# Loading the residual stream from one DMA queue instead of two, at the start of a fused decoder layer

## The chip, the cores and the metric

The kernel runs on one core of one Trainium2 chip. The metric is the device time of one execution in microseconds (us). A profile of one execution lists every instruction and every DMA of that core; its times count from the start of the span, and MB are 10^6 bytes.

## What is computed

One layer of a decoder trunk on x of shape (1, 1024, 1024) in float32, D = 1024 and 1024 tokens:

```python
mod = silu(c) @ w_ada + b_ada                     # 6 vectors of D
sh1, sc1, ga1, sh2, sc2, ga2 = split(mod, 6)
h = rmsnorm(x, g_attn) * (1 + sc1) + sh1
proj = h @ w_in                                   # 2760 columns
out_a = dilated_mixture(qa, ka, va)               # 8 heads
out_b = sparse_attention(qi, ki, wi, qb, ckv)     # 8 heads, indexer and top-256
x = x + ga1 * (concat(out_a, out_b) @ w_out)
h2 = rmsnorm(x, g_ffn) * (1 + sc2) + sh2
x = x + ga2 * ((silu(gate) * up) @ w_down)        # gate, up = h2 @ w_gu
return rmsnorm(x, g_final)
```

Only the first lines bear on the change: the first modulation (sh1 and sc1), the norm of x, and the first columns of `h @ w_in`.

## The kernel before, in words

All tensors are float32. Products that need the precision are made of three matmuls over high and low parts (hh and hl of h, wh and wl of a weight); this is `mm3`, and L366, L367 and L368 are its three matmuls.

**The start, which the change touches.** ScalarE (`A` in the code, ACT in the profile) issues five small loads: c into `cc` (L229), then g_attn, g_ffn, kv_norm_g and b_ada into `gst` (L232 to L235). `load_half(1)` and then `load_half(0)` load the two halves of x, 512 tokens each, into a tile `xi` of 128 partitions. A half is four DMAs (`load_x`, L106 to L111), one for each group of 32 partitions, in the order 0, 2, 1, 3; each has 512 KB in 128 rows of 4 KB. The four are dealt out in turn to the engines named in a tuple: SyncE (SP) takes groups 0 and 1 of each half, ScalarE groups 2 and 3.

Behind that, SyncE alone issues what follows. `mod1_load(0)` (L276) is eight DMAs of 256 KB each, in rows of 1 KB, into the tile `va`: a quarter of the columns of w_ada that make sh1 and sc1. Then come the first two pieces of w_in (`wraw`, L209, 512 KB each in rows of 512 bytes), `mod1_load(1)` into `score` (eight DMAs of 256 KB), and, as the buffers come free, groups 2 and 3 and further pieces of w_in.

The computation over them: ScalarE makes silu(c) with one Exp (L239) behind its DMA issues. `norm_half` takes the sums of squares of a half of x, two of its four pieces on ScalarE (L264) and two on VectorE (L261), then the root (L144) and the scaling of `xi` by it, half 1 on VectorE (L269), half 0 on GpSimd (L271). `mod1(g)` multiplies silu(c) with group g of the weights on TensorE (L288), copies the sums from PSUM on ScalarE (`macc`, L291), adds them up on TensorE (L295), and VectorE finishes two columns each of `a1` and `s1` (L299, L301). `h_part(k, half)` transposes one column block of one half of x (L307), scales and shifts it on ScalarE (L309), and rounds it to `hh` (L310); the rest goes to `hl` (L312). `w_cols` makes `wh` of a piece of w_in on ScalarE (L212) and `wl` on GpSimd (L215). The first products over `hh` are those of the indexer (`qi_proj`).

**What sets the order.** Each engine works through its instructions in order, and a DMA issue that must wait holds up what stands behind it on the same engine. Which instruction stands where on an engine is planned before the run: the program is built under `tile.TileContext(nc, schedule_with_timeline_sim=True)`, which orders each engine's instructions along a simulated timeline, and it also places the semaphores. Only in some later places does the code fix an order by hand (`tc.issue_after`), as where the bits of the top-k search on VectorE alternate with the projections on TensorE.

After the start come the indexer's scores (L418 to L424), the top-k search on VectorE beside the other projections, the two kinds of attention, the output projection, and the FFN with its final norm. None of them is touched.

Of the kernel before, what the change touches and what calls it, by code (L numbers as in the profile page):

```python
# [68 lines left out]
def hybrid_block(ctx, tc, x, c, w_ada, b_ada, g_attn, w_in, kv_norm_g, w_uk, w_uv, w_out, g_ffn,  # L69
                 w_gu, w_down, g_final, lnm, out, dbg=None):  # L70
    nc = tc.nc
    V, A, G, PE = nc.vector, nc.scalar, nc.gpsimd, nc.tensor
# [32 lines left out]
    def load_x(engs, xi, t0, t1):  # L105

        for i, r in enumerate((0, 2, 1, 3)):
            src = bass.AP(tensor=x.tensor, offset=x.offset + (t0 * P + r) * D,
                          ap=[[4 * D, 32], [P * D, t1 - t0], [1, D]])
            last = engs[i % len(engs)].dma_start(xi[32 * r:32 * r + 32], src)  # L110
        return last  # L111
# [110 lines left out]
    xh = {}  # L222

    def load_half(half):
        xh[half] = stg.tile([P, 4, D], F32, name="xi", tag="xi", bufs=2)
        load_x((nc.sync, A), xh[half], half * 4, half * 4 + 4)

    cc = const.tile([P, 8], F32, name="cc")
    A.dma_start(cc, c.rearrange("b (p k) -> (b p) k", k=8))  # L229
# [4 lines left out]
    A.dma_start(gst[16:17], kv_norm_g)  # L234
    A.dma_start(gst[32:80], b_ada.rearrange("b (k p) -> (b k) p", p=P))  # L235
    load_half(1)
    load_half(0)
    ce = const.tile([P, 8], F32, name="ce")
    A.activation(ce, cc, AF.Exp, scale=-1.0)  # L239
# [1305 lines left out]
```

## Time and profile before

| | us |
|---|---|
| median of 3 runs | 1442.23 |
| lowest, highest | 1440.17, 1444.19 |
| the profiled execution | 1437.92 |
| its span, first to last instruction | 1436.1 |

The profile lists, for each engine, when an instruction ran and what ended the idle time before it. PE is TensorE's matmul, PEld its weight load, DVE VectorE, ACT ScalarE, POOL GpSimd; SPq and ACTq are instructions that issue DMAs on SyncE and ScalarE. In the view of the DMA queues, q1 is the queue that SyncE issues on and q10 the one of ScalarE; sixteen DMA engines serve both, and a packet is one row of a transfer.

### The profile page before, as it was taken

The numbers are of one execution on the slowest core, as the hardware profiler recorded it, in microseconds if no ns is written. First come the engines' busy times: TensorE is split into PE (matmuls) and PEld (weight loads), VectorE is DVE, ScalarE is ACT, GpSimd is POOL, SyncE is SP. The second block draws the span as 40 slices with busy tenths as digits, with TensorE's granted clock in tenths as the row PEclk, the third lists the DMA queues.
The fourth block names the chain that finished last, engine by engine and source line by source line (L and its number), as shares of the span: only waits on it lengthen the run. The fifth ranks groups of instructions, "written<-read, shape, count | busy, mean of one in ns | idle before, by whom it ended". The sixth has DMA issues, their size and how long they took to land.

```text
span 1436.1 us, 20358 instructions
## 1 busy us (share of the span) xinstructions
PE 1297.0 (90%) x7477; PEld 1033.9 (72%) x7477; DVE 1016.3 (71%) x1754; ACT 598.8 (42%) x1217; POOL 674.9 (47%) x454
## 2 busy tenths in 40 slices
PE   2999898999878899999869999999999998888894
PEld 0566776798666677787748888888888886766773
DVE  4136899999887477644987545554545569999997
ACT  3435546461456565613763333333333223223334
POOL 1650311324330598122676444445544436487865
PEclk9999898999989999999979999999999999999997
DMA  9723124233311444273423222222223281404004
GB/s 240 238 75 117 30 67 125 91 101 95 126 52 54 147 142 119 76 227 114 161 79 98 89 88 81 66 88 81 81 88 96 87 322 46 154 23 154 0 1 118
DMA packets 133018, 152.11 MB, mean 106 GB/s; under 512 B 9715, under 2 KB 95540, under 8 KB 132918
## 3 DMA queue, kind: packets, MB, share of 16 engines
q1 hardware_dynamic: 122160, 129.56, 29.8%
q0 software_dynamic: 4672, 15.73, 2.9%
q10 hardware_dynamic: 6086, 5.52, 1.5%
q8 instruction: 59, 0.97, 0.3%
q14 instruction: 41, 0.34, 0.1%
HBM read 115.65 MB, written 34.60 MB: 105 GB/s over the span
## 4 chain that ended last, share of the span: by engine, by line
PE 49%; DVE 29%; POOL 8%; DMA 6%; issue 5%; ACT 3%; SPq 1%; DVEq 0%; ACTq 0%; POOLq 0%
DVE score L620 7%; PE mm L1258 6%; PE mm L1256 6%; PE mm L1257 6%; PE tp L1256 3%; PE tp L1258 3%; PE tp L1257 3%; PE mm L366 3%; PE mm L368 3%; PE mm L367 2%; PE o L762 2%; DVE yacc L1376 2%; PE mm L762 2%; PE tp L762 2%; DVE score L424 2%
## 5 line engine op out<-in xcount | busy, mean ns | idle before, releaser
L1240 ACT ACTIVATE wo<-f 128x512 fp32r<-128x512 f32 x124 | 78.0, 631 | 178.0 <-PE mm L1258 78.8
L1241 DVE TENSOR_TENSOR wo<-f,wo 128x512 fp32r<-128x512 f32 x124 | 102.7, 831 | 43.8 <-ACT wo L1240 41.9
L366 PE MATMUL mm<-hh,wl 128*128 128x512 f32 (+2 forms) x288 | 111.7, 389 | 0.0
L367 PE MATMUL mm<-hh,wh 128*128 128x512 f32 (+2 forms) x288 | 111.2, 387 | 0.0
L368 PE MATMUL mm<-hl,wh 128*128 128x512 f32 (+2 forms) x288 | 108.1, 385 | 0.0
L214 POOL TENSOR_SCALAR wh<-wraw 128x1024 fp32r<-128x1024 f32 (+1 forms) x20 | 20.3, 1032 | 132.6 <-PE mm L368 82.3
L366 PE MATMUL mm<-wo,wo 128*128 128x512 f32 x148 | 59.0, 398 | 10.1 <-DVE wo L1366 10.1
L215 POOL TENSOR_TENSOR wl<-wraw,wh 128x1024 fp32r<-128x1024 f32 (+1 forms) x22 | 52.6, 2410 | 29.8 <-ACT ry L144 29.7
L366 PEld LDWEIGHTS mm<-hh,wl 128*128 128x128 f32 (+1 forms) x288 | 54.4, 189 | 15.2 <-issue 2.8
L368 PEld LDWEIGHTS mm<-hl,wh 128*128 128x128 f32 (+1 forms) x288 | 53.7, 188 | 14.0 <-issue 2.2
L367 PEld LDWEIGHTS mm<-hh,wh 128*128 128x128 f32 (+1 forms) x288 | 54.6, 190 | 11.5 <-issue 1.1
L368 PE MATMUL mm<-wo,wo 128*128 128x512 f32 x148 | 56.9, 393 | 1.7 <-DVE wo L1366 1.7
L367 PE MATMUL mm<-wo,wo 128*128 128x512 f32 x148 | 58.2, 393 | 0.0
L793 ACT ACTIVATE ttB<-ttB,mn 128x128 f32<-128x128 f32 (+7 forms) x64 | 49.1, 768 | 15.5 <-DVE mn L789 14.9
L1366 DVE TENSOR_TENSOR wo<-f,wo 128x1536 fp32r<-128x1536 f32 (+1 forms) x17 | 55.1, 3246 | 0.0
L1310 POOL TENSOR_TENSOR f<-f 128x512 f32<-128x512 f32 x15 | 19.8, 1322 | 74.2 <-ACT f L1309 74.2
L366 PE MATMUL mm<-wo,ml 128*128 128x512 f32 x128 | 51.6, 403 | 1.8 <-DVE ml L1109 1.8
L762 PE MATMUL tp<-ident,ttB 128*128 128x128 f32 x288 | 43.6, 294 | 10.2 <-ACT ptB L808 9.7
L620 DVE TENSOR_SCALAR_CACHE_REDUCE score<-kl,sc 128x1024 bf16<-128x1024 uint16 (+2 forms) x48 | 52.3, 1140 | 0.0
L620 DVE TENSOR_SCALAR_CACHE_REDUCE score<-ka,sc 128x768 bf16<-128x768 int16 (+2 forms) x48 | 52.3, 1139 | 0.0
L367 PE MATMUL mm<-wo,mh 128*128 128x512 f32 x128 | 51.0, 398 | 0.0
L368 PE MATMUL mm<-wo,mh 128*128 128x512 f32 x128 | 50.9, 398 | 0.0
(469 smaller groups left out, 4238.7 us busy)
## 6 DMA issues: line engine op xcount, KB each, us to landing
f<-in_w_gu_dram SPq DMA_DIRECT2D x44, 512.0 KB, 3.8
spg<-f POOLq DMA_DIRECT2D x44, 256.0 KB, 2.8
wraw<-in_w_in_dram SPq DMA_DIRECT2D x21, 512.0 KB, 4.0
f<-spg SPq DMA_DIRECT2D x33, 256.0 KB, 3.0
va<-in_w_ada_dram SPq DMA_DIRECT2D x16, 512.0 KB, 4.2
wlm<-in_w_ada_dram SPq DMA_DIRECT2D x32, 256.0 KB, 2.7
f<-in_w_down_dram SPq DMA_DIRECT2D x23, 256.0 KB, 3.1
more<-in_w_down_dram SPq DMA_DIRECT2D x21, 256.0 KB, 5.4
```

Source lines behind the costliest of these rows:

```text
L215: G.tensor_tensor(lo, raw, hi.bitcast(F32), op=OP.subtract)
L366: PE.matmul(p, al, bh, start=(j == 0), stop=False)
L367: PE.matmul(p, ah, bh, start=False, stop=False)
L368: PE.matmul(p, ah, bl, start=False, stop=(j == n - 1))
L620: V.tensor_scalar(mask(t, u), keys[:, seg[t]], z[:, i:i + 1], 0.0, op0=OP.is_lt, op1=OP.add, accum_out=cnt[:, i:i + 1])
L762: pe_last[0] = op(*args, **kw)
L1240: A.activation(h_, src, AF.Copy)
L1241: V.tensor_tensor(l_, src, h_.bitcast(F32), op=OP.subtract)
L1256: PE.matmul(p, w[1][:, k], a[0][:, k], start=(k == 0), stop=False)
L1257: PE.matmul(p, w[0][:, k], a[0][:, k], start=False, stop=False)
L1258: PE.matmul(p, w[0][:, k], a[1][:, k], start=False, stop=(k == 3))
L1366: V.tensor_tensor(l_, x, h_.bitcast(F32), op=OP.subtract)
```

## The change

The tuple of engines in `load_half` loses SyncE. All eight DMAs of x are issued by ScalarE, behind its five small loads, and SyncE's first DMA is the first one of `mod1_load(0)`. Sizes, order of the eight among themselves, tiles and everything else in the code stay.

```diff
     def load_half(half):
         xh[half] = stg.tile([P, 4, D], F32, name="xi", tag="xi", bufs=2)
-        load_x((nc.sync, A), xh[half], half * 4, half * 4 + 4)
+        load_x((A,), xh[half], half * 4, half * 4 + 4)
```

## Rows read from the trace of the kernel before

**Rows 1.** The page's head and its part on busy time: time, share, instructions
```profile
span 1436.1 us, 20358 instructions
PE 1297.0 (90%) x7477; PEld 1033.9 (72%) x7477; DVE 1016.3 (71%) x1754; ACT 598.8 (42%) x1217; POOL 674.9 (47%) x454
```

**Rows 2.** Windows: stretch, length, busy us of each engine, PEclk, DMA share, GB/s
```profile
0.00:36.00 36.00, 8.76 (x33) 2.47 (x33) 15.40 (x49) 11.46 (x18) 5.53 (x12) 0.98 1.02 240
36.00:110.00 74.00, 70.34 (x385) 47.31 (x384) 21.22 (x42) 29.37 (x51) 40.52 (x29) 0.98 0.54 162
```

**Rows 3.** Timeline of SyncE: start, us, engine, line, instruction, output and input, count
```profile
0.74 1.80 SPq L110 DMA_DIRECT2D xi<-in_x_dram  x4
6.04 20.03 SPq L276 DMA_DIRECT2D va<-in_w_ada_dram  x8
26.11 1.09 SPq L209 DMA_DIRECT2D wraw<-in_w_in_dram  x2
```

**Rows 4.** Timeline of ScalarE to 36 us; in brackets the idle time before, its releaser
```profile
5.75 0.32 ACTq L235 DMA_DIRECT2D gst<-in_b_ada_dram  x1
6.36 7.81 ACTq L110 DMA_DIRECT2D xi<-in_x_dram  x4
14.20 1.28 ACT L239 ACT_TABLE_LOAD   x1 [14.20 <-DMA gst<-in_b_ada_dram]
...
19.67 1.06 ACT L264 ACTIVATE sq<-xi 128x1024 bf16<-128x1024 f32 x1 [3.97 <-DMA xi<-in_x_dram]
...
25.22 1.06 ACT L264 ACTIVATE sq<-xi 128x1024 bf16<-128x1024 f32 x1 [1.84 <-DMA xi<-in_x_dram]
...
27.22 0.19 ACT L264 ACTIVATION_READ_ACCUMULATOR sq<-xi 128x1 f32 x1
30.71 0.60 ACT L291 ACTIVATE macc<-o 128x512 f32<-128x512 f32 x1 [3.31 <-PE o L288]
31.31 1.06 ACT L212 ACTIVATE wh<-wraw 128x1024 fp32r<-128x1024 f32 x1
...
33.10 1.06 ACT L212 ACTIVATE wh<-wraw 128x1024 fp32r<-128x1024 f32 x1 [0.64 <-DMA wraw<-in_w_in_dram]
34.06 0.76 ACT L309 ACTIVATE h<-tp,mcol 128x512 f32<-128x512 f32 x1
```

**Rows 5.** Who SyncE's issues waited for, to 80 us: total us, times, longest
```profile
SPq L276 <- DMA xi<-in_x_dram: 6.3, 3, 2.2
SPq L276 <- DMA cc<-in_c_dram: 3.5, 1, 3.5
```

**Rows 6.** DMA queues from 6 to 12 us: packets, MB, share of 16 engines
```profile
q1 hardware_dynamic: 327, 1.21, 104.3%
q10 hardware_dynamic: 18, 0.00, 0.7%
```

**Rows 7.** DMA queues from 15 to 24 us
```profile
q10 hardware_dynamic: 453, 1.66, 82.5%
q1 hardware_dynamic: 449, 0.43, 23.4%
```

**Rows 8.** DMA queues from 36 to 50 us, weights alone
```profile
q1 hardware_dynamic: 5066, 4.88, 109.5%
```

**Rows 9.** Windows again: the first 3 us, and a stretch of w_in alone
```profile
0.00:3.00 3.00, 0.00 (x0) 0.00 (x0) 1.28 (x13) 0.00 (x0) 2.04 (x10) 1.00 0.37 62
30.00:33.00 3.00, 2.22 (x16) 1.31 (x12) 0.55 (x6) 1.75 (x3) 0.49 (x1) 1.00 1.16 297
```

**Rows 10.** Timeline of all engines around the first products
```profile
29.62 1.05 PE L288 MATMUL o<-va,tab 128*32 128x512 f32 x4 [0.48 <-DMA va<-in_w_ada_dram]
...
34.69 1.90 PE L288 MATMUL o<-score,tab 128*32 128x512 f32 x4 [1.78 <-DMA score<-in_w_ada_dram]
...
37.69 4.41 POOL L271 TENSOR_SCALAR xi<-xi,rr 128x1024 f32<-128x1024 f32 x4 [0.53 <-DVE rr L151]
```

**Rows 11.** Who TensorE waited for, whole span: total us, times, longest
```profile
PE tp L1186 <- DVE f L1179: 12.9, 2, 7.2
```

## The prediction, made before the changed kernel was run

> **What bounds the kernel now.** The page comes first: TensorE is busy for 1297.0 of 1436.1 us [rows 1], so a change at the start is worth what it moves the moment from which TensorE has work without a break. The windows view gives that moment: until 36 us TensorE is busy for 8.76 us while the DMA engines' share is 1.02, and from 36 to 110 us it is busy for 70.34 of 74 us [rows 2]. The start is bound by loads, what follows by TensorE, and a shift at 36 us reaches the end about one for one.
>
> The timelines of the two issuing engines show how the loads stand. SyncE issues its four DMAs of x from 0.74, then eight weight DMAs spread from 6.04 to 26.07, then w_in [rows 3]. ScalarE issues its four DMAs of x from 6.36 to 14.17, and only then loads the table for the Exp [rows 4]. The spreading is waiting: SyncE's weight issues waited 3.5 us for the landing of `cc` and 6.3 us in three waits for landings of x [rows 5]. I read it so that each issue waits for a DMA several places earlier to land, whichever queue that was on.
>
> The queue view gives three rates. From 6 to 12 us only q1 moves anything, x in 4 KB rows, 1.21 MB, or 0.202 MB/us; q10 gets 18 packets, though ScalarE issued x at 6.36 [rows 6]. From 15 to 24 us q10 carries x and q1 weights in 1 KB rows: 453 packets against 449, so one each in turn, and 1.66 against 0.43 MB, or 0.184 and 0.048 MB/us [rows 7]. Weights alone go at 4.88 MB in 14 us, 0.348 MB/us [rows 8]; w_in at 0.297 [rows 9]. So x is the slow kind, and beside weights it takes four fifths.
>
> **The change, part by part.** Sizes are from the code: x 8 x 512 KB = 4.19 MB, first weights 8 x 256 KB = 2.10 MB, first w_in 2 x 512 KB = 1.05 MB. The same bytes must come; what changes is their order.
>
> Issues. SyncE loses four issues (1.80 us [rows 3]) that stand before all weights; ScalarE gets four more at idle time. I cost both at nothing: until 36 us TensorE waits for bytes. If that cover were gone, the price would be some 2 us.
>
> Weights start first. The first 3 us moved at 62 GB/s, 0.19 MB [rows 9], which at 0.202 MB/us puts the first bytes at 2.1 us. From there weights run alone until x joins. ScalarE's x waits behind its five small loads; it began at 6.36 because the fifth of these left only at 5.75 [rows 4]. Now the first four weight DMAs, 1.05 MB, are through at 2.1 + 1.05/0.348 = 5.1, the small loads among them. I take first bytes of x at 5.5 (bounds: 4, with the small loads landing at once, and 12, as before). By then 3.4 x 0.348 = 1.18 MB of weights are in.
>
> From 5.5 both flow as in rows 7. Half 1 takes 2.10/0.184 = 11.4 us, to 16.9, half 0 the same again, to 28.3. Before, q10 ran dry at about 24.1 and ScalarE squared half 0 at 25.22 [rows 4]; that lag of 1.1 us gives half 1 at 18.0 (19.67 before [rows 4]) and **half 0 at 29.4, against 25.2**. The other 0.92 MB of weights needs 0.92/0.048 = 19.2 us: in at 24.7, usable at 25.8, where the last matmul of the first modulation waited for them until 29.62 [rows 10]. Then w_in: about 0.1 MB beside the end of x, the other 0.95 MB at 0.297 in 3.2 us, to 31.5, usable at about 32.2 with a lag of 0.7, against 33.10 [rows 4]. The gain on bytes is 0.9 us.
>
> The added wait on ScalarE. Its last issue of x can leave only when the fourth DMA of half 1 has landed (18.0), and the table load stands behind it: 18.3 to 19.6, against 14.20 to 15.48 [rows 4]. Then the Exp, and the squares of half 1 from 19.8, where they stood at 19.67: no loss. The first modulation's matmuls wait for silu(c), at about 20.7; sixteen at 1.90/4 = 0.48 us [rows 10] end at 28.4, before ScalarE can use them, as follows.
>
> ScalarE works in order: squares of half 0, then `macc`, then two `wh`, then `h`. The squares took from 25.22 to 27.41, 2.19 us, and it then idled 3.31 us until `macc` [rows 4]. That idle time hides 3.3 us of a later half 0: up to a landing at 28.5 nothing moves, behind it all does. At 29.4 the squares end at 31.6, `macc` is 0.9 us later, the first `wh` starts at 32.2 and the second 1.15 us later (31.31 to 33.10 less the wait of 0.64 for w_in, which is gone [rows 4]), at 33.35; it takes 1.06, so `h` starts at 34.4 against 34.06: 0.3 us later. On the other side the second group's weights follow w_in and come 0.9 us earlier, and TensorE waited for them at 34.69 [rows 10]. GpSimd's `wl` stands behind `wh`, and its scaling of half 0 behind that: 37.69 [rows 10] becomes 38.6, 0.9 us later, and the transposes of half 0 wait for it.
>
> Sum: between 0.9 us gained on weights and 0.9 us lost through half 0. I take +0.3, the shift of `h`, which both paths meet. The profiled execution took 1437.92, its span and 1.8 us around; that makes 1438.2. The median is 4.3 us above that execution, and from it I forecast 1442.5. A measurement of this kernel can tell about 0.3% from no change, 4.3 us: this is none.
>
> [...]
>
> **The rivals.** *x comes later still: slower.* Place: half 0 in front of `macc` on ScalarE. It decides once half 0 lands after 28.5, and passes the 0.3% bound at 32.8. If the engines alternated by DMA instead of by packet, 512 KB of x to 256 KB of weights, x would get two thirds of 0.232, 0.155 MB/us, and 4.19 MB would take 27.0 us: 5.5 + 27.0 + 1.1 = 33.6, 5.1 us past the point, 1447. At worst SyncE's queue holds ScalarE's back, as rows 6 look: 2.10 MB of weights (6.0 us), w_in (3.5) and the second group (6.0) first, so x from 17.6, alone at 0.202 for 20.8 us, usable at 39.5: 11.0 us past the point, 1453. For it: rows 6. Against it: rows 7, with DMAs of both queues waiting and packets one for one. Chance 0.12. [...]
>
> *The weights' head start counts: a little faster.* If `macc` is planned before the squares of half 0, it runs when the matmuls end at 28.4, and the second `wh` waits for w_in alone, 0.9 us earlier. The rest of the path then gains that 0.9, 1441.3. For it: the plan orders by a simulated timeline, in which x and weights have moved. Against it: the order now, and GpSimd's late half 0. Chance 0.20, still within 0.3%.
>
> *The plan changes far from the start.* The order on every engine comes from that timeline; a shift of a microsecond at the start can exchange neighbours anywhere. One exchange costs or saves about a long wait of TensorE: the longest later one is 7.2 us [rows 11]. Faster: 1442.2 - 7.2 = 1435, chance 0.22. Slower: 1449.4, chance 0.08. For it: nothing in the code fixes the order at the start. Against it: TensorE is full from 36 us on, and a plan that is only moved in time keeps its order.
>
> *Nothing happens*: the same bytes by 32 us, whatever the queue. That is within the forecast.
>
> **The numbers.** Forecast 0.38 and the little gain 0.20 lie within 0.3%: same 0.58. Faster 0.22 is the changed plan. Slower 0.20 is late x with 0.12 and the changed plan with 0.08. The range holds the changed plan on both sides and the first price of a late x: 1435 to 1450. Only the held-back queue and larger changes of plan lie outside.
>
> **What would show it.** SyncE's first weight issue at 0.74, and q1 at 1 KB rows in the first 6 us; ScalarE's x from 4 to 5 us on, its last issue near 18, the table load behind it; q10 dry near 28; squares of half 0 on ScalarE near 29.4; `macc` near 31.6; TensorE's first product within 1 us of 36.5. If x starts near 12 or runs well under 0.184 MB/us, the sharing is wrong; if `macc` stands before the squares, the order is; if TensorE's start is right and the end is off by more than 2 us, the plan has changed further on.

## The result, and the profile after

| | before | after |
|---|---|---|
| median of 9 runs each, side by side (us) | 1440.17 | 1452.01 |
| lowest, highest (us) | 1436.80, 1450.86 | 1446.69, 1455.63 |
| the profiled execution (us) | 1437.92 | 1446.69 |

The ratio is 1.0068, 95% interval 1.0041 to 1.0095: slower by 0.68%, 9.8 us of 1442. It is estimated from the single executions, those more than 1.5% above the fastest of their kernel left out (here none), and is not the quotient of the two medians, 1.0082. The forecast was no change, and its range ended at 1450. The profiled execution of the changed kernel is the fastest of its nine, so its span understates the loss; the start, where the kernels differ, is what to read in it.

Two windows of the changed kernel (columns as in [rows 2]), then one of the kernel before, from the second of [rows 2]:

```profile
0.00:36.00 36.00, 4.53 (x17) 1.05 (x17) 4.79 (x26) 3.85 (x6) 3.21 (x11) 0.94 0.99 224
36.00:60.00 24.00, 19.36 (x73) 7.14 (x74) 13.10 (x31) 11.66 (x21) 10.76 (x8) 0.67 0.98 309
```

```profile
36.00:60.00 24.00, 23.56 (x118) 11.13 (x116) 3.62 (x9) 10.37 (x17) 15.38 (x12) 0.95 0.99 310
```

TensorE's busy time in the first 60 us falls from 32.32 to 23.89 us: 8.4 us of its work are pushed behind 60 us. Fewer bytes have come by 36 us (224 against 240 GB/s, 8.06 against 8.64 MB), and TensorE's clock is granted at 0.67 between 36 and 60 us. That is a mean of its two levels: after TensorE had stood idle from 28.43 us, the clock was at 0.50 from 31.5 to 51.9 us, and at 1.00 from there to 110 us.

Which moment carries the shift on? `hh` is the high part of `h` that the projections read, made in sixteen pieces. One row of it for the kernel before, then after (name, count, ns min/median/max, first and last start in us):

```profile
L310 ACT ACTIVATE hh<-h x16: 622/630/634, 34.9 to 78.2; 128x512 fp32r<-128x512 f32 x16
```

```profile
L310 ACT ACTIVATE hh<-h x16: 613/627/642, 47.4 to 88.9; 128x512 fp32r<-128x512 f32 x16
```

The first `hh` is 12.5 us later and the last 10.7. The first row of the top-k search (L620) starts at 200.5 us instead of 190.4, 10.1 us later. The loss is made before 90 us and then carried along.

Where does it come from? SyncE, ScalarE and VectorE in the changed kernel's timeline:

```profile
0.74 7.30 SPq L276 DMA_DIRECT2D va<-in_w_ada_dram  x8
8.86 11.76 SPq L209 DMA_DIRECT2D wraw<-in_w_in_dram  x2
21.20 16.62 SPq L276 DMA_DIRECT2D score<-in_w_ada_dram  x8
```

```profile
4.17 17.66 ACTq L110 DMA_DIRECT2D xi<-in_x_dram  x8
21.86 1.28 ACT L239 ACT_TABLE_LOAD   x1 [21.86 <-DMA xi<-in_x_dram]
...
33.64 1.06 ACT L212 ACTIVATE wh<-wraw 128x1024 fp32r<-128x1024 f32 x1 [10.28 <-DMA wraw<-in_w_in_dram]
34.60 1.04 ACT L264 ACTIVATE sq<-xi 128x1024 bf16<-128x1024 f32 x1
...
36.68 1.04 ACT L212 ACTIVATE wh<-wraw 128x1024 fp32r<-128x1024 f32 x1
37.63 0.57 ACT L291 ACTIVATE macc<-o 128x512 f32<-128x512 f32 x1
...
45.91 0.78 ACT L309 ACTIVATE h<-tp,mcol 128x512 f32<-128x512 f32 x1 [3.04 <-DVE ss L261]
```

```profile
35.77 2.50 DVE L261 CUSTOM_DVE_ANT_0 sq<-xi 128x1024 bf16<-128x1024 f32 x1 [10.27 <-ACT sq L264]
```

Set these beside [rows 3, 4]. SyncE sends all eight weight DMAs by 8.04 and the first piece of w_in at 8.86, and ScalarE's x starts behind its small loads and spreads to 21.83. And the planner has written **another order on ScalarE**: the first `wh` now stands ahead of all the squares, and `macc` behind the second `wh`. Half 1 of x has landed, but ScalarE waits 10.28 us for w_in; VectorE, which shares the squares, waits 10.27 us for ScalarE. TensorE (idle time and its releaser in brackets) had its first modulation done at 28.43, and then waited 9.82 us for `macc`; its first product starts at 48.12, not 36.5:

```profile
24.27 4.16 PE L288 MATMUL o<-va,tab 128*32 128x512 f32 x16 [14.55 <-DVE tab L281]
38.25 1.87 PE L295 MATMUL tp<-ones,macc 128*128 128x1 f32 x8 [9.82 <-ACT macc L291]
...
48.12 0.77 PE L366 MATMUL mm<-hh,wl 128*128 128x512 f32 x1 [1.07 <-ACT hh L310]
```

The chain of work that ended last says it near its start in three pieces (start, us, what), a single DMA being the long one:

```profile
3.10 5.74 DMA va<-in_w_ada_dram
8.86 24.76 DMA wraw<-in_w_in_dram
33.64 1.06 ACT wh L212
```

Two things have thus changed, the loads and ScalarE's order. Each could be the cause, and the low clock a third.

### The profile page after: what moved, and what is told of

Its sections match the earlier page's. It is cut to its first block, busy times and chain, and to the rows that moved or that the text cites. A ratio compares the mean times of both kernels' runs of the same rounds, so it can differ in the third digit from the quotient of the medians.

```text
span 1444.9 us, 20363 instructions
## 1 busy us (share of the span) xinstructions
PE 1301.7 (90%) x7477; PEld 1038.2 (72%) x7477; DVE 1015.5 (70%) x1754; ACT 598.5 (41%) x1217; POOL 676.1 (47%) x454
## 4 chain that ended last, share of the span: by engine, by line
PE 52%; DVE 31%; DMA 5%; POOL 4%; issue 4%; ACT 4%; SPq 0%; DVEq 0%; ACTq 0%; POOLq 0%
DVE score L620 7%; PE mm L1256 6%; PE mm L1257 6%; PE mm L1258 6%; PE o L762 3%; PE tp L1256 3%; PE tp L1258 3%; PE tp L1257 3%; PE mm L366 3%; PE mm L368 3%; PE mm L762 3%; PE mm L367 3%; PE tp L762 2%; DVE yacc L1376 2%; DVE wo L1366 2%
## 5 line engine op out<-in xcount | busy, mean ns | idle before, releaser
L366 PE MATMUL mm<-wo,wo 128*128 128x512 f32 x148 | 60.4, 408 | 8.6 <-DVE wo L1366 8.6
L368 PE MATMUL mm<-wo,wo 128*128 128x512 f32 x148 | 58.2, 402 | 1.7 <-DVE wo L1366 1.7
L367 PE MATMUL mm<-wo,wo 128*128 128x512 f32 x148 | 59.4, 401 | 0.0
L620 DVE TENSOR_SCALAR_CACHE_REDUCE score<-ka,sc 128x768 bf16<-128x768 int16 (+2 forms) x48 | 52.3, 1140 | 0.0
L620 DVE TENSOR_SCALAR_CACHE_REDUCE score<-kl,sc 128x1024 bf16<-128x1024 uint16 (+2 forms) x48 | 52.3, 1140 | 0.0
L424 DVE SCALAR_TENSOR_TENSOR score<-rl,wi,score 128x512 f32<-128x512 f32 (+2 forms) x70 | 48.3, 747 | 3.1 <-ACT rl L418 2.0
L367 PE MATMUL mm<-wo,mh 128*128 128x512 f32 x128 | 50.3, 393 | 0.0
```

Source lines behind the costliest of these rows:

```text
L366: PE.matmul(p, al, bh, start=(j == 0), stop=False)
L367: PE.matmul(p, ah, bh, start=False, stop=False)
L368: PE.matmul(p, ah, bl, start=False, stop=(j == n - 1))
L620: V.tensor_scalar(mask(t, u), keys[:, seg[t]], z[:, i:i + 1], 0.0, op0=OP.is_lt, op1=OP.add, accum_out=cnt[:, i:i + 1])
```

## The experiments

The letters of theories in an expectation are its own. The table has all twelve beside the changed kernel: the ratio to the kernel before, with its interval, and the start of the last `hh` in the profiled execution (78.2 before, 88.9 after).

| run | x on | ratio | last `hh` |
|---|---|---|---|
| the changed kernel | one queue | 1.0068 [1.0041, 1.0095] | 88.9 |
| squares first | one | 1.0032 [1.0011, 1.0053] | 83.2 |
| `macc`, `wh` first | one | 1.0100 [1.0067, 1.0133] | 86.4 |
| half 0 behind squares | one | 1.0103 [1.0068, 1.0138] | 90.5 |
| warm TensorE | one | 1.0088 [1.0065, 1.0111] | 88.5 |
| small loads moved, squares first | one | 0.9994 [0.9975, 1.0013] | 77.4 |
| small loads moved | one | 1.0003 [0.9987, 1.0019] | 77.6 |
| `wh` first | two | 0.9997 [0.9970, 1.0025] | 79.6 |
| order of after | two | 1.0015 [0.9991, 1.0038] | 81.0 |
| x before small loads | two | 1.0021 [0.9993, 1.0050] | 79.9 |
| small loads moved | two | 0.9983 [0.9966, 0.9999] | 72.3 |
| the same again | two | 0.9993 [0.9969, 1.0016] | 72.1 |
| same half at once | two | 1.0037 [1.0013, 1.0060] | 77.7 |

### Is it ScalarE's order? The order mended, the loads kept

The changed kernel, with both conversions of w_in collected and written behind the squares of half 0.

```diff
-    wqi = [w_cols([(C_QI, P), (C_QI + P, P)], True)]
+    converts = []
+    wqi = [w_cols([(C_QI, P), (C_QI + P, P)], True, converts)]
...
+    with tc.issue_after(sq_on_act[0].ins):
+        for convert in converts:
+            convert()
```

> x stays on ScalarE's queue alone; only ScalarE's order is changed back: the two conversions of w_in (wh) stand behind the squares of both halves of x. Theory A (the loss is the order that was planned on ScalarE: it waits for w_in from 23.4 to 33.6 us in front of the squares of half 1): the squares of half 1 start by 24, the first h by 36 instead of 45.9, and the time returns to 1440 to 1444 where the kernel before is at 1440, at least 6 us under the changed kernel. Theory B (the loss is the bytes: x and w_in land late, whatever the order): the first h stays above 42 and the time within 3 us of the changed kernel's, about 1450. Theory C (the loss is made by exchanged neighbours in later stages): the first h comes early, but the end stays some 8 us behind it.

Measured 1446.21 us, 1.0032: about half the loss is gone. The first `h` comes at 39.77, between the times that theories A and B name. ScalarE's timeline, and who TensorE waited for between 30 and 50 us (total, times, longest):

```profile
23.38 1.04 ACT L272 ACTIVATE sq<-xi 128x1024 bf16<-128x1024 f32 x1
...
28.86 0.60 ACT L299 ACTIVATE macc<-o 128x512 f32<-128x512 f32 x1 [3.31 <-PE o L296]
...
32.81 1.06 ACT L272 ACTIVATE sq<-xi 128x1024 bf16<-128x1024 f32 x1 [1.84 <-DMA xi<-in_x_dram]
...
34.91 1.99 ACT L214 ACTIVATE wh<-wraw 128x1024 fp32r<-128x1024 f32 x2
...
39.77 0.78 ACT L317 ACTIVATE h<-tp,mcol 128x512 f32<-128x512 f32 x1 [2.87 <-PE tp L315]
```

```profile
PE o L296 <- DMA score<-in_w_ada_dram: 4.5, 3, 3.1
```

`macc` comes even earlier than before (28.86 against 30.71), so weights ahead of x did pay there. But half 0 is squared 7.6 us later than before (32.81 against 25.22), and the second group of weights keeps TensorE waiting for 4.5 us. Which of the two decides, the chain that ended last tells:

```profile
15.73 19.81 DMA wraw<-in_w_in_dram
...
37.50 5.89 DMA score<-in_w_ada_dram
43.53 1.07 PE o L296 x4
```

It runs over w_in and not over x. SyncE's last issues of the second group stand behind the landing of w_in at 35.54, so the last four matmuls over that group start at 43.53, where they started at 40.19 in the kernel before. The last `hh` is 5.0 us late: that part is the loads'. The other 5.7 us came with the order.

### The order alone, with the loads of before

Two runs on the kernel before: the first conversion of w_in written ahead of the squares of half 1, with `macc` still in front; and the changed kernel's full order (`wh`, squares of half 1, `wh`, `macc`, squares of half 0).

```diff
+    first_wh = converts[0]()
...
-    norm_half(1)
+    with tc.issue_after(first_wh.ins):
+        norm_half(1)
+    converts[1]()
```

> The kernel before, x on both queues, with one thing taken from the changed kernel: on ScalarE the first conversion of w_in stands ahead of the squares of half 1. Theory A: the conversion can't start before w_in has landed (about 31 us in the kernel before), the squares move from 19.7 to about 32.4, the first h from 34.1 to 42 or 44, and the time rises by 6 to 10 us, to 1446 to 1450. Theory B: x and weights land as before, so the time stays within 2 us of 1440.

> x on both queues as before; ScalarE's order at the start is set by hand to the changed kernel's: first conversion, squares of half 1, second conversion, and only then the sums of the first modulation. Those sums then move from 30.7 to about 35 us, TensorE stands idle from 30.7 to 36 and its clock may fall as it did in the changed kernel. If this order is the larger part of the loss whatever the loads, the time rises by 4 to 7 us, to 1446 to 1449. If the loss needs both, late w_in and this order, it stays within 2 us of the kernel before.

Measured 0.9997 and 1.0015, neither distinguishable from 1. In the first, `h` starts 10 us late (44.35) at no cost that the time shows: TensorE runs the second group's modulation meanwhile, and the last `hh` starts at 79.6. The second puts `h` at 45.59, as late as in the changed kernel, and its last `hh` at 81.0, 2.8 us late instead of 10.7. So **a late first `h` is no measure of the loss**, and the order by itself explains about 2.8 us of lateness. In these profiled executions loads and order cost 5.0 + 2.8 = 7.8 us each alone and 10.7 together: about 3 us come only with both. That w_in is late just where the order waits for it would explain them; no run separates it.

The reverse was tried too, the changed kernel's loads with the first run's order (`macc`, `wh`, squares):

> x on ScalarE's queue alone; ScalarE's order at the start is set by hand to that of the second experiment (sums of the first modulation, then the first conversion, the squares of half 1, the second conversion, the squares of half 0), which cost nothing with x on both queues. If late bytes alone cost (theory B, the 0.3% that the first experiment kept), it comes out as the first experiment did, 1444 to 1447 where the kernel before is at 1442. If the place of the sums behind both conversions was what cost the rest, this order saves 3 to 6 us against the changed kernel. If instead any order with a conversion ahead of the squares costs when w_in lands at 33 us, it stays at 1449 to 1452.

The median is 1460.04, but its ten runs spread from 1444.74 to 1471.43, far wider than those of the changed kernel, and the profiled one was the fastest of them (last `hh` at 86.4). Why it spreads stays open. It does not rescue the change.

### Less beside each other: half 0 held back

The changed kernel, with half 0 of x and both conversions of w_in placed only behind the squares of half 1.

```diff
-    load_half(0)
...
+    with tc.issue_after(sq_on_act[1].ins):
+        load_half(0)
```

> x on ScalarE's queue alone, but half 0 is issued behind the squares of half 1, so the weights and w_in share the DMA engines with 2.1 MB of x instead of 4.2 first; the conversions of w_in stand behind the squares of half 1. Theory A with the loads as priced: half 1 lands by 18 to 20, w_in near 25, the first h by 32; half 0 lands only near 40 and its transposes follow. The time is 1436 to 1444. Theory B: the loss is x's lateness, half 0 is later than in the changed kernel, and the time is at or above 1450.

Measured 1.0103. `macc` gains (23.14 against 28.86), but half 0 is issued only from 30.68 to 34.01, though the squares of half 1 ended at 25.81: ScalarE idled 8.23 us until its next instruction, by the profile for a weight DMA. VectorE, which waits for half 0 itself, squares it at 47.58; ScalarE does at 50.86, behind two more `macc` that now stand ahead. Holding half 0 back in this way costs more than sharing did.

### Is it TensorE's clock?

The changed kernel with 70 small products of the identity behind the first modulation's, so that TensorE does not idle there.

```diff
+        if g == 0:
+            warm = mm_tile("mm")
+            for j in range(70):
+                with tc.issue_after(last_mod.ins):
+                    last_mod = PE.matmul(warm[:, :P], ident, ident, start=True, stop=True)
```

> The changed kernel with 70 small matmuls of the identity added on TensorE behind the first modulation's, into a bank that nobody reads; they fill most of the stretch from 28.4 to 38.3 us in which TensorE waits for ScalarE. The waits and loads stay. If the low granted clock (0.50 from 31.5 to 51.9 us in the changed kernel, 11.4 us of TensorE's busy time in it) is what the idle stretch costs, the clock stays at 1.00 and the time falls by 3 to 6 us, to 1446 to 1449. If TensorE only waits in that time, whatever its clock, the time stays within 2 us of the changed kernel's 1452.

The windows are those of the changed kernel, the granted clock the first number behind the last bracket:

```profile
0.00:36.00 36.00, 12.40 (x91) 9.40 (x92) 5.41 (x26) 4.47 (x7) 3.82 (x11) 1.00 0.98 227
36.00:60.00 24.00, 19.49 (x138) 13.55 (x138) 12.70 (x30) 11.49 (x21) 10.17 (x8) 0.86 0.97 288
```

The clock rises from 0.67 to 0.86 (and from 0.94 to 1.00 before 36 us), and the time does not fall: last `hh` at 88.5, 1.0088. But the products ran past the gap that they were to fill:

```profile
27.67 15.90 PE L294 MATMUL mm<-ident 128*128 128x128 f32 x140
43.41 0.95 PE L300 MATMUL tp<-ones,macc 128*128 128x1 f32 x8
```

`macc` was done at 37.58, yet the sums over it start at 43.41, 5.2 us later than in the changed kernel (38.25). What the higher clock gave may have gone there, so this run does not settle what the low clock costs. That the clock is not the whole cause, the first experiment shows: there it was granted at 1.00 from 24 to 60 us, and 5.0 us of the loss remained. What it has in the other 5.7 stays open.

### What in the loads? The place of x and of the small loads

First the kernel before, with ScalarE issuing x ahead of its small loads:

```diff
+    load_half(1)
     A.dma_start(cc, c.rearrange("b (p k) -> (b p) k", k=8))
+    load_half(0)
...
-    load_half(1)
-    load_half(0)
```

> The kernel before, x on both queues, but ScalarE issues its DMAs of x ahead of its small loads, so that both queues carry x from the first microsecond, SyncE partitions 0 to 63 and ScalarE 64 to 127. If 0.2 MB/us is what a load into 32 partitions can reach and two such loads add up, the 4.2 MB of x land by about 14 us instead of 25 and the first products come up to 8 us earlier (time 1432 to 1438). If 0.2 MB/us is the limit of 4 KB rows, x lands at 23 to 25 as before and the time stays within 3 us of 1440.

x landed early, but the last small load left only at 20.03. VectorE then copied out what TensorE had made of it at 31.52, behind its squares and the scaling of half 1, and the first modulation waited for that copy until 31.81: 1.0021, no gain. The small loads have to be early too. So the next runs issue them from GpSimd, first on the kernel before:

```diff
-    A.dma_start(cc, c.rearrange("b (p k) -> (b p) k", k=8))
+    G.dma_start(cc, c.rearrange("b (p k) -> (b p) k", k=8))
...
-    A.dma_start(gst[32:80], b_ada.rearrange("b (k p) -> (b k) p", p=P))
+    G.dma_start(gst[32:80], b_ada.rearrange("b (k p) -> (b k) p", p=P))
```

> The other way round from the change: x on both queues as before, and ScalarE's five small loads moved to GpSimd's queue, so that both queues carry x from the first microsecond. In the third experiment two loads of x side by side went at about 0.29 MB/us against 0.20 alone, but the small loads and silu(c) came late. Here they come early: x should land by 17 us, the first weights by 24, w_in by 27, all some 6 us earlier than before. If the loads bound the start, the last of the sixteen parts of h is done 4 to 6 us earlier and the time is 1436 to 1439 where the kernel before is at 1442. If TensorE's own work bounds the start from 36 us on, the gain is under 2 us.

Then on the changed kernel, once in the order of the first experiment and once with no other edit; with no other edit the planner writes the squares first by itself.

> The changed kernel with both conversions of w_in behind the squares of half 0 on ScalarE (as in the run that put the squares first) and the five small loads on GpSimd's queue: x alone on ScalarE's queue from the first microsecond, and no small load ahead of it. Theory A (one queue moves x at 0.15 to 0.20 MB/us whatever stands ahead of it): x, 4.19 MB, lands no earlier than 24 us (0.20 from 3 us, nothing beside it) and about 29 us at 0.155 beside the weights, 10 us or more behind the two-queue kernel with the same small loads; the time is 1.001 to 1.004. Theory C (x was late because it started at 4 to 5 us behind the small loads): x lands 4 us earlier than in the run that put the squares first, as does the last h, and the time falls to 0.998 to 1.0005.

> The changed kernel with one edit, the five small loads on GpSimd's queue, and nothing forced on ScalarE: with the small loads off ScalarE's queue the planner itself writes the squares of both halves ahead of the conversions of w_in and macc behind them. Theory C (the loss of the change is that x starts behind the small loads and beside weights that have a head start, and that the planner then puts the first conversion ahead of all squares; x on one queue costs nothing by itself): last hh at 76 to 80 us, as in the run with the forced order and the same loads, time 0.997 to 1.0015 of before. Theory A (one queue for x loses by itself, and the last run was low by chance): 1.002 to 1.005.

**One edit brings the changed kernel back to the time of the kernel before**: 1.0003 with x on one queue. Its ScalarE, and its `hh`:

```profile
0.73 16.13 ACTq L110 DMA_DIRECT2D xi<-in_x_dram  x8
...
18.30 1.04 ACT L264 ACTIVATE sq<-xi 128x1024 bf16<-128x1024 f32 x1
...
27.96 1.06 ACT L264 ACTIVATE sq<-xi 128x1024 bf16<-128x1024 f32 x1 [5.76 <-DMA xi<-in_x_dram]
...
31.66 1.06 ACT L212 ACTIVATE wh<-wraw 128x1024 fp32r<-128x1024 f32 x1 [1.52 <-DMA wraw<-in_w_in_dram]
```

```profile
L310 ACT ACTIVATE hh<-h x16: 622/630/634, 39.1 to 77.6; 128x512 fp32r<-128x512 f32 x16
```

The order isn't all that does it: with the squares first by force in both, moving the small loads takes the last `hh` from 83.2 to 77.4. The queues from 3 to 10 us (packets, MB, share) show the difference, first in the changed kernel, then with the small loads moved:

```profile
q1 hardware_dynamic: 1308, 1.26, 60.4%
q10 hardware_dynamic: 228, 0.55, 40.7%
```

```profile
q10 hardware_dynamic: 309, 1.13, 71.1%
q1 hardware_dynamic: 510, 0.49, 33.8%
```

In the changed kernel the weights ran ahead, 1.26 MB in seven microseconds, and x got 0.55 MB; with x on the queue from 0.73 it gets twice that. The weights' lead buys nothing that lasts, since the first modulation can't start before silu(c), at 24.27, and w_in, issued at 8.86, lands 24.76 us later, behind the rest of the weights and beside x. With x ahead, w_in leaves at 26.96 behind the first weights and is used at 31.66, two microseconds earlier than where it was issued eighteen earlier. The last matmuls over the second group follow: they start at 40.23, as in the kernel before (40.19), where they start at 43.53 with the squares first and at 49.25 in the changed kernel.

The edit does not cancel the change alone. Made on the kernel before, it brings the last `hh` from 78.2 to 72.3, so with the small loads moved the step from two queues to one still costs 5.3 us there, against 10.7 without.

(The profiled execution of this run has the long span of 1455.9 us, against a median of 1440.91, though its last `hh` is as early as 77.6. Executions of one kernel, 1436.68 to 1457.79 us here, can differ that much after the start, which is why the runs are compared by ratio and by `hh`, not by span; here L620 starts at 191.1, as early as in the kernel before.)

### Two queues or two halves of the partitions?

With the small loads on GpSimd and x on both queues, 0.285 MB/us flowed from 3 to 10 us, against 0.213 when x was alone on SyncE's queue in the kernel before. Either two queues are faster, or it matters that SyncE's groups (partitions 0 to 63) and ScalarE's (64 to 127) lie in different halves. The test deals the groups so that both queues write the same half:

```diff
-        for i, r in enumerate((0, 2, 1, 3)):
+        for i, r in enumerate((0, 1, 2, 3)):
```

> The kernel before with its five small loads on GpSimd's queue, and the four 32-row groups of each half dealt to the queues in the order 0, 1, 2, 3 instead of 0, 2, 1, 3: the two queues then carry neighbouring groups of partitions (0 to 31 beside 64 to 95 as before becomes 0 to 31 beside 32 to 63 in the first pair). Theory A (what carries 0.285 MB/us between 3 and 10 us is two queues side by side, whichever partitions): the same rate of 0.27 to 0.29, half 1 landed by 11 to 12 us, time as with the small loads alone moved, 0.9965 to 1.0. Theory B (it is that the two pieces lie in different halves of the partitions): the rate of 3 to 10 us falls towards the 0.20 to 0.25 of one queue, half 1 lands at 13 us or later, and the gain is gone or halved.

> The kernel before with its five small loads on GpSimd's queue once more, in five rounds, beside the two others of this call: if the gain of the first time (0.9983, 1.0 all but reached) is real, the ratio is 0.997 to 0.9995 with an interval below 1; if it was the chance of three rounds, the interval lies on both sides of 1.

The queues from 3 to 10 us, different halves first, then the same half:

```profile
q10 hardware_dynamic: 270, 1.03, 53.3%
q1 hardware_dynamic: 265, 0.95, 49.8%
```

```profile
q10 hardware_dynamic: 200, 0.75, 51.9%
q1 hardware_dynamic: 201, 0.76, 51.3%
```

1.98 MB against 1.51 MB: two queues into one half went no faster than the one of the kernel before (0.217 against 0.213 MB/us). Different halves gave 1.11 + 1.04 MB in the repeat. Half 1 is squared at 14.15 instead of 11.62. The time of the same-half kernel, 1.0037, is more than its start explains (last `hh` at 77.7): the edit also reorders a later load of x (L1124), and what that costs was not separated.

The two-halves version starts 6 us earlier than the kernel before and 5 earlier than the one-edit kernel (last `hh` at 72.3 and 72.1), but L620 only 3.6 and 3.9 us earlier, and the ratios are 0.9983 and 0.9993, the second with an interval on both sides of 1. It has the earliest start of all, and that it beats the kernel before is not settled; nor is what the one queue then costs in time, since 1.0003 and 0.9983 or 0.9993 have intervals that overlap.

## Why the prediction was wrong, step by step

*What bounds the kernel.* Right for a loss: 10.7 us at the last `hh` became 9.8 us of time, 5.0 became 4.6 (0.32%). For a gain it fell short: 6 us earlier became 2.5 (0.17%) and 1.0 (0.07%), with intervals that reach up to 4.9. And the moment to watch was not the first product but the last `hh`.

*The weights' head start.* Right as to what it does: the first modulation waited for silu(c) and not for weights, and its matmuls ended at 28.43, where the forecast has 28.4. The agreement is luck: silu(c) let them start at 24.27 instead of 20.7, and the sixteen took 4.16 us instead of 7.7. x was issued from 4.17 on ScalarE, and its first bytes came at about 6 us (from 5 to 6 us q10 has no packet, from 6 to 7 it has 98), where the forecast has 5.5.

*The share of x.* Right beside the weights, and too early at both ends. From 10 to 30 us x went at 3.61 MB, 0.181 MB/us, against 0.184, and packets were about equal in number, 411 of x to 380 of q1 from 12 to 20 us. But until 10 us x got 0.55 MB, where 4.5 us at 0.184 would have made 0.83, and from 30 to 32 us 32 packets of it were still to come, where the forecast has it through at 28.3. The last issue of x ended at 21.83 instead of 18, the table load stood at 21.86 instead of 18.3, and half 0 was squared at 32.81 in the right order, not 29.4: 3.4 us were mis-sized. The first rival, "x comes later still", has 33.6 for it and 1447, which is where the kernel with the squares first came out, 1.0032 x 1442.2 = 1446.8. That is luck too: the turns by DMA and the steady 0.155 MB/us that gave the price were not what happened, and the chain that ended last in that kernel runs over w_in.

The order in time shows the turns that were taken: in the kernel before, q1 has 16 packets from 19.90 to 20.05 us, none until 20.25 and 16 again until 20.40, with 16 of q10 from 19.95 to 20.25, as if each of the sixteen engines took one of each in turn.

*Nothing happens.* "The same bytes by 32 us, whatever the queue" did not come: by then the changed kernel had moved 6.89 MB, the kernel before 7.30. With the small loads moved the times of the two kernels agree, on one queue 1.0003, on two 0.9983 and 0.9993; their last `hh`, 77.6 against 72.3 and 72.1, don't.

*w_in and what stands behind it.* This step failed: "the second group's weights follow w_in and come 0.9 us earlier". w_in was forecast usable at 32.2, and the first `wh` ran at 33.64. With the squares first, the second piece of w_in landed at 35.54, SyncE's last issues of the second group waited for it (in the changed kernel, too, issues of that group waited for w_in, 3.0 us in two waits), and the last matmuls over that group started 3.3 us later than before. The prediction had read from [rows 5] that an issue waits for a DMA several places earlier, and did not apply it to these issues.

*ScalarE's order.* The second failure, and about the other half of the loss: "ScalarE works in order: squares of half 0, then `macc`, then two `wh`, then `h`". The text took this order over though it names the planner's timeline as what sets it, and in its rivals looked for a changed plan only far from the start, or with `macc` ahead. It listed "if `macc` stands before the squares, the order is [wrong]"; in fact `wh` stood before them. That the planner did so because w_in's issue had moved up to 8.86 is argued, not shown; shown is that with the small loads elsewhere, which puts w_in's issue back to 26.96, it writes the squares first.

*Chances.* Slower had 0.20, as two separate cases, a late x and a changed plan. Both came, from the same edit, and their costs added, though the plan changed at the start and not far from it, where the rival had looked. Here the plan changed with the loads.

## What to carry to other kernels

Moving a load to another queue moves what stands behind it on both: ask what the freed queue now sends early, whether anyone can use it yet, and what it takes from the transfer that is needed first. Where a planner writes the order, a step that takes the old order over is a rival of its own, with its price; here it was about half the loss. Compare variants at the last piece of the stage (here the last `hh`), not the first, and not by the span of one execution.

## What the runs showed of the hardware

Two queues that write 32-partition groups in different halves of the partitions moved 0.285 and 0.308 MB/us of x and small loads between 3 and 10 us, two that write the same half 0.217, one alone into one half 0.213.

A queue of short rows beside one of long rows got packets, not bytes, in about equal number: from 28 to 30 us in the changed kernel 98 packets of w_in (512 bytes, 0.05 MB) beside 99 of x (4 KB, 0.39 MB). From 24 to 28 us it got more, 347 against 193. w_in's 512 KB took 24.76 us from issue to landing there, of which more than half passed behind the first weights on its own queue (from 20 to 22 us that queue still moved rows of 1 KB, 0.12 MB in 123 packets); issued behind x, the median was 6.0 us.
